# S5's tables in two sets of buffers with a later transpose, six tables loaded in the first FFN, and MoBA's bias rows written in 32 pieces

## The chip, the cores and the metric

One core of a Trainium2 chip runs the whole forward pass as one program. The metric is the device time of one execution in microseconds (us); lower is better. The core has five engines with an instruction stream each: PE (TensorE, matrix products; its weight loads are listed as PEld), DVE (VectorE), ACT (ScalarE), POOL (GpSimd) and SP (SyncE, which here only issues transfers). Each engine works through its own stream in order and waits on semaphores for the others. DRAM transfers (DMA) are issued from the queues of SP, ACT and POOL and run on 16 DMA engines. SBUF is the on-chip memory of 128 partitions, PSUM the accumulators that PE writes.

## What is computed

A model of four layers, width 1024, on one sequence of 256 tokens, in float32. Each layer is a feed-forward block (FFN, 1024 to 2816 to 1024), a mixer, and a second FFN. The mixers are S5 (a diagonal linear recurrence of 64 groups, 64 complex states and 16 channels each), HGRN2, GDN and MoBA (attention with a bias that depends on the distance, taken from a table of 32 buckets by 8 heads).

```python
def _swiglu(x, w_gate, w_up, w_down):
    return (jax.nn.silu(x @ w_gate) * (x @ w_up)) @ w_down

def _s5_mixer(u, lam_re, lam_im, log_dt, b_re, b_im, c_re, c_im, d_skip, w_glu):
    ...
    lam_bar = jnp.exp(lam * dt)
    b_bar = ((lam_bar - 1.0) / lam)[..., None] * lax.complex(b_re, b_im)
    bu = jnp.einsum('blgh,gph->lbgp', ug, b_bar)
    _, h = lax.associative_scan(combine, (a, bu), axis=0)      # h[l] = lam_bar * h[l-1] + bu[l]
    y = jnp.einsum('lbgp,ghp->blgh', h, c).real.reshape(bsz, L, D_MODEL)
    y = jax.nn.gelu(y + d_skip * u)
    val, gate = jnp.split(y @ w_glu, 2, axis=-1)
    return val * jax.nn.sigmoid(gate)

for i in range(DEPTH):                                          # 4 layers: S5, HGRN2, GDN, MoBA
    x = x + 0.5 * _swiglu(_rms(x, norm_g[i, 0]), ffn_w_gate[i, 0], ffn_w_up[i, 0], ffn_w_down[i, 0])
    x = x + mixer_i(_rms(x, norm_g[i, 1]))
    x = x + 0.5 * _swiglu(_rms(x, norm_g[i, 2]), ffn_w_gate[i, 1], ffn_w_up[i, 1], ffn_w_down[i, 1])
return _rms(x, final_norm_g)
```

## The kernel before

**Parts.** The program runs twelve parts in a row (PARTS): the FFN (0,0), S5, the FFN (0,1), the FFN (1,0), HGRN, and so on; MoBA is the last mixer. FFN (l,0) stands ahead of the mixer of layer l and FFN (l,1) behind it.

**Products.** Each float32 product is made of three matmuls of 512 columns (`wide`, lines 347 to 349), because a weight block is cut in two parts, `hi` and `lo = raw - hi`. `Weights.pump` loads raw blocks on SP's queue (L71, four raw buffers), ACT casts `hi` (L88) and VectorE subtracts `lo` (L91, 128x1024, both inputs in SBUF). An FFN is 66 steps of 12 such matmuls, 792 in all: 11 blocks of four steps for gate and up, then 22 steps for down. `hhl` is the hidden state, so the matmuls of gate and up read `xhl` and those of down read `hhl`. L459 stands once in each FFN near its start, L484 writes its result at the end. `step()` in `ffn` runs once per step; at its end it also calls `next(self.prep)`, at odd steps before the 32nd and at each step before the 60th.

**S5's tables.** `self.prep` is a generator (`s5_prep`) which lays the making of S5's matrices beside the first FFN, the only FFN that has it. It makes eight tables `j`, for 8 groups each. For one table POOL issues six operations of 128x512 (L732, L733 and L734, twice) into the second half of the buffer `s5e`, the halves `ebs`; VectorE issues three of 128x1024 (L737, L738, L740) into its first half `eo`; PE makes a block of 16 small matmuls (L746) from `eo` and eight transposes (L760) of `ebs`; ACT copies the transposes out of PSUM (L761); and SP writes `s5_out` (L741), for every fourth table `s5_k` (L754, 8 transfers), and `s5_in` (L762, 2 transfers) to DRAM. There is one buffer `s5e`, so POOL's L733 of the next table waits for the transposes of this one, and PE's transposes wait for POOL's L734. There are two `yield`s in a table. Behind the tables `s5_phases` makes the powers of the recurrence for the first half on POOL.

**S5.** `s5()` reads the tables back from DRAM with `load`, twelve tables of 1 MB (four each of `in`, `t` and `out`) in five buffers (tags A to E) that the preparation used before. `in` tables go into the scan's input (`inward`), `t` tables (L804, eight transfers each) and `out` tables into the output `y` (`to_y`, whose matmuls are listed at L882). POOL makes the phases of the second half and `xr` (L943), then two of the second scan's products (L898); VectorE's second scan follows and ends in the transposes L952, whose result PE transposes at L955. `busy` (L253) lays idle matmuls into a wait.

**The bias.** `moba_bias`, called in the first FFN after the preparation, that is FFN (0,1), behind its gate and up blocks in the program's text, reads the bias table, builds a row of 384 values per head on POOL, and writes it 128 times to DRAM, as 8x128x384 values (1536 KB), in one transfer on ACT's queue (L1719). A scheduler of the framework places the instructions on each engine by their dependences and a cost model, so an instruction's place need not be that of its line.

```python
pb = [back[:, n, h].unsqueeze(3).to_broadcast(wh) for n in range(2)]
g(tb[:, :4], b1[:, h].unsqueeze(2).to_broadcast(wh), pb[0], op=OP.mult)
g(split(eb), b2[:, h].unsqueeze(2).to_broadcast(wh), pb[1], op=OP.mult)
g(split(eb), split(eb), tb[:, :4], op=OP.add)
```

## Time and profile before

| what | value |
|---|---|
| median of 3 runs | 2255.6 us (2252.84 to 2257.62) |
| the profiled execution | 2255.48 us, its span in the profile 2253.7 us |
| mean granted TensorE clock | 0.982 of full speed |
| PE busy | 2147.5 us, 95% of the span, 11480 instructions |
| PEld busy | 1771.5 us, 79% |
| DVE busy | 1464.5 us, 65%, 2412 instructions |
| ACT busy | 1159.8 us, 51% |
| POOL busy | 288.1 us, 13%, 305 instructions |
| DMA | 389.63 MB, 173 GB/s in the mean |
| chain that ended last | PE 80%, DVE 9%, ACT 4%, DMA 3%, POOL 2% |

Busy shares are means over stages that differ. The chain of waits and the waits of PE tell where the end is set; the first 300 us and the FFN behind S5 are the two places that the change touches. All times below are from the start of the span.

### The profile page before, as it was taken

The numbers are of one execution on the slowest core, as the hardware profiler recorded it, in microseconds if no ns is written. First come the engines' busy times: TensorE is split into PE (matmuls) and PEld (weight loads), VectorE is DVE, ScalarE is ACT, GpSimd is POOL, SyncE is SP. The second block draws the span as 40 slices with busy tenths as digits, with TensorE's granted clock in tenths as the row PEclk, the third lists the DMA queues.
The fourth block names the chain that finished last, engine by engine and source line by source line (L and its number), as shares of the span: only waits on it lengthen the run. The fifth ranks groups of instructions, "written<-read, shape, count | busy, mean of one in ns | idle before, by whom it ended". The sixth has DMA issues, their size and how long they took to land.

```text
span 2253.7 us, 30309 instructions
## 1 busy us (share of the span) xinstructions
PE 2147.5 (95%) x11480; PEld 1771.5 (79%) x11480; DVE 1464.5 (65%) x2412; ACT 1159.8 (51%) x1876; POOL 288.1 (13%) x305
## 2 busy tenths in 40 slices
PE   8989888999999999999999888899999999999998
PEld 6767566888888888887888766777888888898886
DVE  7986675556555877557554888887655555666555
ACT  6444344445454755445444566764544544555443
POOL 0598600000000000001000422322000000000000
PEclk9999899999999999999999999999999999999999
DMA  8656956655555645555655433233555655555553
GB/s 254 195 188 203 239 185 166 191 195 179 186 179 185 198 132 169 187 190 167 190 185 175 144 100 104 85 113 121 179 187 172 202 186 178 196 168 178 187 177 103
DMA packets 317906, 389.63 MB, mean 173 GB/s; under 512 B 14192, under 2 KB 247856, under 8 KB 316736
## 3 DMA queue, kind: packets, MB, share of 16 engines
q1 hardware_dynamic: 314768, 383.92, 53.7%
q10 hardware_dynamic: 2800, 3.68, 0.9%
q8 instruction: 90, 1.47, 0.3%
q14 instruction: 56, 0.46, 0.1%
q0 software_dynamic: 192, 0.10, 0.0%
HBM read 375.65 MB, written 12.01 MB: 172 GB/s over the span
## 4 chain that ended last, share of the span: by engine, by line
PE 80%; DVE 9%; ACT 4%; DMA 3%; POOL 2%; issue 1%; SPq 0%; ACTq 0%; DVEq 0%; POOLq 0%
PE acc L349 23%; PE acc L347 23%; PE acc L348 23%; DVE lo L91 2%; PE acc L315 2%; PE acc L316 2%; PE acc L317 2%; PE aux L439 2%; DVE cy L1395 1%; DMA raw<-in_ffn_w_up_dram 1%; ACT hi L88 1%; PE aux L230 1%; POOL s5e L733 1%; POOL s5e L734 1%; POOL s5tmp L732 1%
## 5 line engine op out<-in xcount | busy, mean ns | idle before, releaser
L91 DVE TENSOR_TENSOR lo<-raw,hi 128x1024 fp32r<-128x1024 f32 x648 | 813.1, 1257 | 585.4 <-ACT hi L88 582.3
L88 ACT CAST hi<-raw 128x1024 fp32r<-128x1024 f32 x681 | 713.1, 1049 | 708.2 <-PE acc L349 657.5
L347 PE MATMUL acc<-hi,xhl 128*128 128x512 f32 x1568 | 627.2, 400 | 9.9 <-ACT hi L88 9.4
L348 PE MATMUL acc<-lo,xhl 128*128 128x512 f32 x1568 | 618.9, 395 | 2.8 <-DVE lo L91 2.7
L349 PE MATMUL acc<-hi,xhl 128*128 128x512 f32 x1568 | 616.9, 394 | 0.0
L347 PEld LDWEIGHTS acc<-hi,xhl 128*128 128x128 f32 x1568 | 297.1, 190 | 73.0 <-ACT hi L88 10.7
L349 PEld LDWEIGHTS acc<-hi,xhl 128*128 128x128 f32 x1568 | 296.9, 189 | 66.6 <-issue 3.1
L348 PEld LDWEIGHTS acc<-lo,xhl 128*128 128x128 f32 x1568 | 297.5, 190 | 64.4 <-DVE lo L91 5.2
L347 PE MATMUL acc<-hi,hhl 128*128 128x512 f32 x704 | 276.9, 393 | 0.0
L349 PE MATMUL acc<-hi,hhl 128*128 128x512 f32 x704 | 276.7, 393 | 0.0
L348 PE MATMUL acc<-lo,hhl 128*128 128x512 f32 x704 | 275.5, 391 | 0.0
L349 PEld LDWEIGHTS acc<-hi,hhl 128*128 128x128 f32 x704 | 132.8, 189 | 27.6
L348 PEld LDWEIGHTS acc<-lo,hhl 128*128 128x128 f32 x704 | 132.9, 189 | 27.4
L347 PEld LDWEIGHTS acc<-hi,hhl 128*128 128x128 f32 x704 | 132.7, 188 | 27.0
L317 PE MATMUL acc<-xhl,lo 128*128 128x256 f32 x520 | 150.2, 291 | 0.0
L316 PE MATMUL acc<-xhl,hi 128*128 128x256 f32 x520 | 149.5, 290 | 0.2 <-DVE xhl L241 0.2
L315 PE MATMUL acc<-xhl,hi 128*128 128x256 f32 x520 | 149.6, 291 | 0.1
L427 ACT ACTIVATE sl<-acc,norm_r 128x256 f32<-128x256 f32 x176 | 83.6, 475 | 107.2 <-PE acc L349 88.9
L91 POOL TENSOR_TENSOR lo<-raw,hi 128x1024 fp32r<-128x1024 f32 x33 | 81.8, 2478 | 342.7 <-ACT hi L88 322.6
L430 DVE TENSOR_TENSOR h<-acc,sl 128x256 f32<-128x256 f32 x176 | 74.0, 420 | 49.8 <-ACT sl L427 49.7
L315 PEld LDWEIGHTS acc<-xhl,hi 128*128 128x128 f32 x520 | 99.6, 193 | 2.6 <-issue 1.7
L316 PEld LDWEIGHTS acc<-xhl,hi 128*128 128x128 f32 x520 | 99.8, 193 | 1.6 <-issue 0.9
(564 smaller groups left out, 2285.7 us busy)
## 6 DMA issues: line engine op xcount, KB each, us to landing
raw<-in_ffn_w_gate_dram SPq DMA_DIRECT2D x174, 512.0 KB, 3.9
raw<-in_ffn_w_up_dram SPq DMA_DIRECT2D x174, 512.0 KB, 4.8
raw<-in_ffn_w_down_dram SPq DMA_DIRECT2D x80, 1024.0 KB, 4.9
raw<-in_gdn_w_in_dram SPq DMA_DIRECT2D x24, 1024.0 KB, 5.2
raw<-in_hg_w_in_dram SPq DMA_DIRECT2D x16, 1024.0 KB, 5.3
raw<-in_moba_w_in_dram SPq DMA_DIRECT2D x12, 1024.0 KB, 5.0
raw<-in_ffn_w_down_dram SPq DMA_DIRECT2D x16, 512.0 KB, 3.7
raw<-in_s_w_glu_dram SPq DMA_DIRECT2D x16, 512.0 KB, 5.2
```

The source lines that it names most:

```text
L88: pin(self.nc.scalar.copy(hi, src))
L91: eng.tensor_tensor(lo, src, hi.bitcast(F32), op=OP.subtract)
L230: nc.tensor.transpose(q[:, j * 128:j * 128 + 128], self.x[:, t, k * 128:k * 128 + 128], self.ident)
L315: t.matmul(p, hi, ah, start=first, stop=False)
L316: t.matmul(p, hi, al, start=False, stop=False)
L317: t.matmul(p, lo, ah, start=False, stop=last)
L347: mm(p, ah, hi[:, j], start=first and j == 0, stop=False)
L348: mm(p, ah, lo[:, j], start=False, stop=False)
L349: mm(p, al, hi[:, j], start=False, stop=last and j == n - 1)
L427: nc.scalar.activation(sl, p[:, :256], AF.Silu, scale=self.r_col[:, t:t + 1])
L430: return nc.vector.tensor_tensor(waiting[-1][1][:, t], p[:, 256:], sl, op=OP.mult)
L439: nc.tensor.transpose(q[:, c:c + 128], h[:, t, f * 128:f * 128 + 128], self.ident)
```

## The change

Three things are done. First, S5's tables alternate between two buffers, `s5e` and `s5f` (a new sixth tag, G), and the transposes of table j-1 (`turned`) are issued with table j, behind its 16 small matmuls; a table has three `yield`s, with two more around the last transposes, and the generator is stepped at odd steps before the 24th and at every step from there on. Second, a new method `s5_load` holds what `load` did, with six tags; the preparation calls it for six tables (`in` 0 to 3, `t` 0 and 1), with the phases of the first half between them, and `load` in `s5()` takes these before it loads others. Third, `moba_bias` is a generator: its first step builds the row, and each of 32 further steps writes 4 of the 128 copies (8x4x384 values, 48 KB) on ACT's queue, kept in program order; `ffn` steps it once per step from the fifth on, and `moba` finishes what is left. Docstrings and unrelated lines do not change.

```diff
--- before.py
+++ after.py
@@ -443,23 +443,26 @@
                 return nc.vector.tensor_tensor(hhl[:, 2 * j:2 * j + 2, 1], q, hh.bitcast(F32), op=OP.subtract)
 
             steps = [0]
+            bias = None
+            if self.prep is None and self.bias is not None:
+                bias = self.bias(pool)
+                self.bias = None
 
             def step():
                 steps[0] += 1
                 n = steps[0]
                 if n % 4 == 1 and waiting and n > 4:
                     turn()
+                if bias is not None and n > 4:
+                    next(bias, None)
                 if self.prep is not None and n > 4:
-                    for _ in range(n % 2 if n < 32 else 1 if n < 60 else 0):
+                    for _ in range(n % 2 if n < 24 else 1):
                         next(self.prep, None)
 
             for j in range(FT // 2):
                 self.product(self.xhl, KT // 2, lambda t, p: evac(j, t, p), tail=0 if j else 4, step=step)
             half = self.small.tile([128, 2], F32, name="half")
             nc.vector.tensor_scalar(half, self.r_col, 0.5, None, op0=OP.mult)
-            if self.prep is None and self.bias is not None:
-                self.bias(pool)
-                self.bias = None
             ahead = self.ahead
 
             def late():
@@ -708,7 +711,9 @@
         for n in range(8):
             nc.gpsimd.tensor_copy(back[:, :, :, n], pw[:, :, :, 8 - n])
         e = pool.tile([128, 16, 128], F32, name="s5e", tag="s5C")
-        eo, ebs = e[:, :8], (e[:, 8:12], e[:, 12:16])
+        more = pool.tile([128, 16, 128], F32, name="s5f", tag="s5G")
+        eos = e[:, :8], more[:, :8]
+        ebs = [(t[:, 8:12], t[:, 12:16]) for t in (e, more)]
         w = [128, 8, 8, 16]
         split = lambda a: a.rearrange("p g (t h) -> p g t h", h=16)
         ta, tb = [tmp[:, c].rearrange("p (g t h) -> p g t h", t=8, h=16) for c in range(2)]
@@ -721,13 +726,23 @@
                                     pattern=[[128 * sign, 2], [0, 4], [-8 * sign, 32]], channel_multiplier=sign)
         self.s5_place = pool.tile([128, 16], F32, name="s5place")[:, :8]
         v.tensor_reduce(self.s5_place, self.ident.rearrange("p (a t) -> p t a", t=8), op=OP.add, axis=mybir.AxisListType.X)
+        def turned(j):
+
+            for n, eb in enumerate(ebs[j % 2]):
+                p = self.aux.tile([128, 512], F32, name="aux")
+                for g in range(4):
+                    nc.tensor.transpose(p[:, g * 128:g * 128 + 128], eb[:, g], self.ident)
+                nc.scalar.copy(et.rearrange("p g c -> p (g c)"), p)
+                dma(as_ap(self.s5_in, (8 * j + 4 * n) * 128, [[8192, 128], [128, 4], [1, 128]]), et)
+
         for j in range(8):
             r = slice(8 * j, 8 * j + 8)
-
-            rs = (slice(8 * j, 8 * j + 4), slice(8 * j + 4, 8 * j + 8))
-            for h, eb in zip(rs, ebs):
+            eo = eos[j % 2]
+
+            for n, eb in enumerate(ebs[j % 2]):
+                h = slice(8 * j + 4 * n, 8 * j + 4 * n + 4)
                 wh = [128, 4, 8, 16]
-                pb = [back[:, n, h].unsqueeze(3).to_broadcast(wh) for n in range(2)]
+                pb = [back[:, m, h].unsqueeze(3).to_broadcast(wh) for m in range(2)]
                 g = nc.gpsimd.tensor_tensor
                 g(tb[:, :4], b1[:, h].unsqueeze(2).to_broadcast(wh), pb[0], op=OP.mult)
                 g(split(eb), b2[:, h].unsqueeze(2).to_broadcast(wh), pb[1], op=OP.mult)
@@ -739,6 +754,7 @@
             yield
             v.tensor_tensor(split(eo), split(eo), ta, op=OP.add)
             dma(as_ap(self.s5_out, j * 1024, [[8192, 128], [128, 8], [1, 128]]), eo)
+            yield
 
             p = self.aux.tile([128, 512], F32, name="aux")
             for g in range(2):
@@ -753,21 +769,26 @@
                         a = q * 32 + g * 16
                         dma(as_ap(self.s5_k, (8 * (j - 3) + 2 * q + g) * 3840 + 112, [[240, 16], [8 * 3840, 4], [1, 128]]),
                             kk[a:a + 16, :, g])
+            if j:
+                turned(j - 1)
             yield
-            for h, eb in zip(rs, ebs):
-                p = self.aux.tile([128, 512], F32, name="aux")
-                for g in range(4):
-                    nc.tensor.transpose(p[:, g * 128:g * 128 + 128], eb[:, g], self.ident)
-                nc.scalar.copy(et.rearrange("p g c -> p (g c)"), p)
-                dma(as_ap(self.s5_in, h.start * 128, [[8192, 128], [128, 4], [1, 128]]), et)
-
+        yield
+        turned(7)
+        yield
+
+        self.s5_tags = ["s5" + c for c in "ABCDEG"]
+        self.s5_tabs = []
         self.s5_turn = pool.tile([128, 2, 16, 32], F32, name="s5turn", tag="s5pw")
-        yield from self.s5_phases(self.s5_turn, 0, pool)
+        phases = self.s5_phases(self.s5_turn, 0, pool)
+        for kind, part in (("in", 0), ("in", 1), ("in", 2), ("in", 3), ("t", 0), ("t", 1)):
+            self.s5_tabs.append(self.s5_load(kind, part))
+            next(phases, None)
+            yield
 
     def s5_phases(self, turn, half, pool):
 
         eng = self.nc.gpsimd
-        t2 = pool.tile([128, 2, 16, 8], F32, name="s5t2", tag="s5F")
+        t2 = self.s5_pool.tile([128, 2, 16, 8], F32, name="s5t2", tag="s5F")
         pin = self.tc.keep_in_program_order
         pin(eng.memset(turn[:, 0, :, 0:1], 1.0))
         pin(eng.memset(turn[:, 1, :, 0:1], 0.0))
@@ -782,6 +803,21 @@
                           [t2[:, c, :, :n] for c in range(2)], eng)
             yield
 
+    def s5_load(self, kind, part):
+
+        tags = self.s5_tags
+        tags.append(tags.pop(0))
+        t = self.s5_pool.tile([128, 16, 128], F32, name="tab", tag=tags[-1])
+        if kind == "t":
+
+            for s in range(8):
+                self.nc.sync.dma_start(t[s * 16:s * 16 + 16],
+                                       as_ap(self.s5_k, part * 16 * 3840 + (7 - s) * 16, [[240, 16], [3840, 16], [1, 128]]))
+        else:
+            src = self.s5_in if kind == "in" else self.s5_out
+            self.nc.sync.dma_start(t, as_ap(src, part * 2048, [[8192, 128], [128, 16], [1, 128]]))
+        return t.rearrange("p (j q g) c -> p j q g c", q=4, g=2)
+
     def s5_token(self, k):
 
         self.nc.vector.transpose(self.s5_u[:, k].rearrange("p g t h -> p t g h"),
@@ -792,21 +828,12 @@
         v = nc.vector
         mm = nc.tensor.matmul
         pin = self.tc.keep_in_program_order
-        tags = ["s5" + c for c in "ABCDE"]
+        tags = self.s5_tags
 
         def load(kind, part):
-
-            tags.append(tags.pop(0))
-            t = self.s5_pool.tile([128, 16, 128], F32, name="tab", tag=tags[-1])
-            if kind == "t":
-
-                for s in range(8):
-                    nc.sync.dma_start(t[s * 16:s * 16 + 16],
-                                      as_ap(self.s5_k, part * 16 * 3840 + (7 - s) * 16, [[240, 16], [3840, 16], [1, 128]]))
-            else:
-                src = self.s5_in if kind == "in" else self.s5_out
-                nc.sync.dma_start(t, as_ap(src, part * 2048, [[8192, 128], [128, 16], [1, 128]]))
-            return t.rearrange("p (j q g) c -> p j q g c", q=4, g=2)
+            if self.s5_tabs:
+                return self.s5_tabs.pop(0)
+            return self.s5_load(kind, part)
 
         with ExitStack() as ctx:
             pool = ctx.enter_context(self.tc.tile_pool(name="s5", bufs=1))
@@ -1716,7 +1743,11 @@
             nc.gpsimd.tensor_copy(row[:, lo:hi], tab[:, b:b + 1].to_broadcast([8, hi - lo]))
 
         self.bias_rows = self.dram.tile([8, 128, 384], F32, name="bias_rows")
-        nc.scalar.dma_start(self.bias_rows, row.rearrange("h (o s) -> h o s", o=1).to_broadcast([8, 128, 384]))
+        for k in range(0, 128, 4):
+            yield
+            self.tc.keep_in_program_order(nc.scalar.dma_start(
+                as_ap(self.bias_rows, k * 384, [[128 * 384, 8], [384, 4], [1, 384]]),
+                row.rearrange("h (o s) -> h o s", o=1).to_broadcast([8, 4, 384])))
 
     def moba(self, i):
         nc = self.nc
@@ -1725,7 +1756,7 @@
         with self.tc.tile_pool(name="moba", bufs=1) as pool, self.tc.tile_pool(name="moba2", bufs=2) as two:
             bt = pool.tile([128, H, L], F32, name="bt")
             if self.bias is not None:
-                self.bias(pool)
+                self.settle(self.bias(pool))
 
             nc.scalar.dma_start(bt, as_ap(self.bias_rows, 127, [[383, 128], [128 * 384, H], [1, L]]))
             qk = pool.tile([128, 2, H, L], F32, name="qk")
```

On POOL, at the start of the tables in the first FFN, the stream before was this (`s5D` and `s5kk` are inputs, `s5tmp` the first product, `s5e` the table buffer):

```order
L709 COPY s5kk<-s5pw 128x128 x8
L732 TENSOR_TENSOR s5tmp<-s5D,s5kk 128x512
L733 TENSOR_TENSOR s5e<-s5D,s5kk 128x512 x2
L734 TENSOR_TENSOR s5e<-s5e,s5tmp 128x512
L732 TENSOR_TENSOR s5tmp<-s5D,s5kk 128x512
L734 TENSOR_TENSOR s5e<-s5e,s5tmp 128x512
```

With the change it is this:

```order
L712 COPY s5kk<-s5pw 128x128 x8
L747 TENSOR_TENSOR s5tmp<-s5D,s5kk 128x512
L748 TENSOR_TENSOR s5e<-s5D,s5kk 128x512 x2
L749 TENSOR_TENSOR s5e<-s5e,s5tmp 128x512
L748 TENSOR_TENSOR s5f<-s5D,s5kk 128x512
L747 TENSOR_TENSOR s5tmp<-s5D,s5kk 128x512
L748 TENSOR_TENSOR s5f<-s5D,s5kk 128x512
L749 TENSOR_TENSOR s5e<-s5e,s5tmp 128x512
```

The same six operations per table remain, 48 in all; writes to the second buffer stand among those to the first. On PE the last transposes of the tables (L760 before, L734 now) stand behind 629 of the FFN's 792 wide matmuls before, and behind 664 with the change.

On SP, at the end of the first FFN and ahead of S5, the stream before was this (`tab` with its number is a table that S5 reads; `raw` blocks of `in_s5_w_glu` are S5's weights):

```order
L741 DMA s5_out_1203<-s5e_1215 128x1024
L754 DMA s5_k_1204<-s5kk_1206 16x4x128 x8
L762 DMA s5_in_1202<-s5tmp_1009 128x512
...
L808 DMA tab_2325<-s5_in_1202 128x2048
L71 DMA raw_2076<-in_s5_w_glu_dram 128x4x256 x2
L808 DMA tab_2344<-s5_in_1202 128x2048
...
L804 DMA tab_2454<-s5_k_1204 16x16x128 x8
L804 DMA tab_2481<-s5_k_1204 16x16x128 x8
L808 DMA tab_2531<-s5_out_1203 128x2048
```

With the change it is this:

```order
L770 DMA s5_k_1118<-s5kk_1120 16x4x128 x8
L736 DMA s5_in_1116<-s5tmp_939 128x512
...
L818 DMA tab_1970<-s5_in_1116 128x2048
L736 DMA s5_in_1116<-s5tmp_939 128x512
...
L818 DMA tab_2055<-s5_in_1116 128x2048
L71 DMA raw_2067<-in_s5_w_glu_dram 128x4x256 x2
L814 DMA tab_2082<-s5_k_1118 16x16x128 x7
L814 DMA tab_2125<-s5_k_1118 16x16x128 x8
L71 DMA raw_2138<-in_s5_w_glu_dram 128x4x256 x2
```

The `in` tables and the first `t` table stood ahead of or among S5's weight loads already, since the scheduler had drawn them forward. The first `in` table now stands ahead of the last writes of `s5_in`, and the second `t` table comes ahead of S5's last weight loads.

On ACT, at the end of S5 and the start of FFN (0,1), the one transfer stood here before (L240 normalises, L88 casts weights):

```order
L246 ACTIVATE junk_3160,ssq_2822<-x_81 128x512
L240 ACTIVATE xhl_2821<-aux_3147,gains_95 128x128
L1719 DMA bias_rows_4161<-row_4133 1024x1x384
L240 ACTIVATE xhl_2821<-aux_3147,gains_95 128x128
L427 ACT_TABLE_LOAD
```

With the change the first pieces stand in the FFN's steps, one per step, between the casts:

```order
L442 CAST hhl_3191<-aux_3296 128x2x256
L1748 DMA bias_rows_3333<-row_3305 8x4x384
L88 CAST hi_3351<-raw_3098 128x1024
L1748 DMA bias_rows_3333<-row_3305 8x4x384
L88 CAST hi_3371<-raw_3202 128x1024
```

Each piece also waits for the semaphore that the fourth piece before it signals, so at most four are under way, and a piece that waits holds up the casts behind it on ACT.

## Rows read from the trace of the kernel before

**Rows 1.** Waits of PE in 0 to 500 us (engine, tile, line <- releaser: total us, times, longest).

```profile
PE acc L882 <- DMA tab<-s_k: 11.6, 3, 5.0
PE aux L760 <- POOL s5e L734: 10.9, 5, 2.7
PE acc L347 <- ACT hi L88: 8.1, 2, 7.4
PE aux L746 <- DVE s5e L740: 4.5, 2, 3.1
```

**Rows 2.** Windows (us, busy of PE, PEld, DVE, ACT, POOL; clock, DMA share, GB/s).

```profile
40.00:80.00 40.00, 38.45 (x191) 30.86 (x190) 38.08 (x128) 25.90 (x38) 5.64 (x9) 1.00 0.56 170
260.00:290.00 30.00, 18.13 (x298) 12.78 (x299) 23.92 (x33) 3.24 (x6) 20.58 (x25) 0.76 1.15 236
```

**Rows 3.** Lines by form, 109.3 to 204.9 us (count | busy us, mean ns | idle before, releaser).

```profile
L91 DVE TENSOR_TENSOR lo<-raw,hi 128x1024 fp32r<-128x1024 f32 x22 | 38.9, 1769 | 16.5 <-ACT hi L88 16.5
L734 POOL TENSOR_TENSOR s5e<-s5e,s5tmp 128x512 f32<-128x512 f32 x16 | 29.6, 1852 | 0.6
L733 POOL TENSOR_TENSOR s5e<-s5D,s5kk 128x512 f32<-128x512 f32 x16 | 27.5, 1736 | 9.8 <-PE aux L760 9.8
L732 POOL TENSOR_TENSOR s5tmp<-s5D,s5kk 128x512 f32<-128x512 f32 x16 | 27.3, 1705 | 1.3
...
L740 DVE TENSOR_TENSOR s5e<-s5e,s5tmp 128x1024 f32<-128x1024 f32 x7 | 13.2, 1883 | 0.1
L738 DVE TENSOR_TENSOR s5e<-s5E,s5pw 128x1024 f32<-128x1024 f32 x7 | 12.8, 1833 | 0.6 <-PE aux L746 0.3 <-DMA s_out<-s5e 0.2
L737 DVE TENSOR_TENSOR s5tmp<-s5E,s5pw 128x1024 f32<-128x1024 f32 x6 | 11.1, 1855 | 0.0
```

**Rows 4.** Timeline of POOL in the tables (start us, us, engine, line, operation).

```profile
109.35 1.05 POOL L732 TENSOR_TENSOR s5tmp<-s5D,s5kk 128x512 f32<-128x512 f32 x1
...
136.11 4.04 POOL L733 TENSOR_TENSOR s5e<-s5D,s5kk 128x512 f32<-128x512 f32 x2
...
169.68 2.07 POOL L733 TENSOR_TENSOR s5e<-s5D,s5kk 128x512 f32<-128x512 f32 x2
171.71 1.28 POOL L734 TENSOR_TENSOR s5e<-s5e,s5tmp 128x512 f32<-128x512 f32 x1
...
202.71 2.13 POOL L734 TENSOR_TENSOR s5e<-s5e,s5tmp 128x512 f32<-128x512 f32 x1
```

**Rows 5.** Timeline of DVE, one table operation with POOL idle.

```profile
182.65 1.22 DVE L737 TENSOR_TENSOR s5tmp<-s5E,s5pw 128x1024 f32<-128x1024 f32 x1
```

**Rows 6.** Timeline of PE, behind the last table and at the FFN's end.

```profile
205.62 0.40 PE L347 MATMUL acc<-hi,hhl 128*128 128x512 f32 x1
...
244.19 0.60 PE L936 MATMUL acc<-zero 128*128 128x512 bf16 x2
```

**Rows 7.** Timeline of POOL, DVE and PE in S5, around the second scan.

```profile
278.63 2.49 POOL L898 TENSOR_TENSOR tb<-inc,turn 128x512 f32<-128x512 f32 x2
...
288.61 1.30 DVE L952 STREAM_TRANSPOSE sc<-S 128x512 f32<-128x512 f32 x2
...
292.01 0.81 PE L955 MATMUL aux<-ident,sc 128*128 128x128 f32 x3
```

**Rows 8.** Lines L459 and L484, 300 to 600 us, and L484, 600 to 900 us (durations, starts).

```profile
L459 DVE TENSOR_SCALAR half<-norm_r x2: 169/169/169, 351.0 to 548.8; 128x2 f32<-128x2 f32 x2
...
L484 DVE SCALAR_TENSOR_TENSOR x<-acc,half,x x4: 744/746/750, 510.4 to 543.3; 128x512 f32<-128x512 f32 x4
...
L484 DVE SCALAR_TENSOR_TENSOR x<-acc,half,x x4: 743/746/751, 697.7 to 730.7; 128x512 f32<-128x512 f32 x4
```

**Rows 9.** Transfers (KB each, us to landing): 345 to 390 us; 0 to 500 us.

```profile
raw<-in_ffn_w_up_dram SPq DMA_DIRECT2D x6, 512.0 KB, 15.1
...
s_in<-s5tmp SPq DMA_DIRECT2D x16, 256.0 KB, 3.0
```

**Rows 10.** Timeline of ACT's queue, the bias transfer's issue.

```profile
350.43 0.79 ACTq L1719 DMA_DIRECT2D bias_rows<-row  x1
```

## The prediction

> **What bounds the kernel now.** I read PE's waits first, then the windows, then the groups of lines in the stretch where the tables are made, then single rows of the timeline. The waits list says where PE stood still in the first 500 us [rows 1]: 11.6 us for S5's `t` tables, 10.9 us in the transposes of the tables for POOL's L734, 8.1 us for a cast on ACT (7.4 of it in one piece), 4.5 us in the small matmuls for VectorE's L740. These are what the three parts of the change aim at. But a wait that is taken away is worth only what no other work takes over, so for each I look at what ends next.
>
> *First FFN, tables.* The tables run from 109.35 to 204.84 us [rows 4], 95.5 us. The reader should see in [rows 3] that L732, L733 and L734 on POOL take about 1.7 to 1.85 us each and VectorE's L91, L737, L738 and L740 about 1.8 to 1.9. The same operations alone are far shorter: on POOL the two L733 at 169.68 take 2.07 us together and L734 1.28, against 4.04 for two L733 at 136.11 [rows 4]; L737 takes 1.22 on VectorE while POOL is idle [rows 5]. So the two engines slow each other when both run. Counted together, there are 48 operations on POOL and 22 + 7 + 7 + 6 = 42 on VectorE [rows 3], 90 in 95.5 us, 1.06 us each, nearly what each takes alone. The two engines behave almost like one, and that one has hardly any room: the waits of PE and POOL's 9.8 us behind PE's transposes [rows 3] lie beside VectorE's half of that work. *S5.* In 260 to 290 us POOL is busy for 20.6 of 30 us and VectorE for 23.9, PE for 18.1 with a granted clock of 0.76 [rows 2]. *The bias.* FFN (0,1) runs from L459 at 351.0 to the last L484 at 543.3, 192.3 us; FFN (1,0), the same work without a bias, from 548.8 to 730.7, 181.9 us [rows 8]. The excess is 10.4 us.
>
> **The sum** is made against the profiled execution, 2255.48 us (its span 2253.7); the median of the runs is 2255.6, so the two can be taken as one.
>
> *1. Tables with a second buffer, PE one step behind.* Nothing is added to the tables' arithmetic: 48 operations on POOL, 24 on VectorE, as many transposes, copies and writes. POOL starts a little later: with the change one more table operation of VectorE stands ahead of POOL's copies, and VectorE has 38.08 us of work in the 40 before [rows 2], so I take about one such operation, 1.14 us (1.22 [rows 5] less what consecutive operations overlap): 110.49. From there VectorE has 17 table operations rather than 20 beside POOL, since three more of them come earlier, but 25 splits rather than 22, because PE uses more weights by then. Again 90 operations at 1.06 us, so 95.5 us: POOL ends at 205.98. What is gained is that PE does not stand by. In the order the last transposes are reached after 664 wide matmuls, not after 629, so 128 and not 163 are left. PE resumed 0.78 us after POOL's end, at 205.62, and the FFN ended at 244.19 [rows 6]: 38.57 us for 163 matmuls, so 30.3 us for 128. The FFN then ends at 205.98 + 0.78 + 30.3 = 237.1 rather than 244.2: **-7.1 us**. Bounds: if every operation costs what it does alone and they strictly follow each other, POOL's 48 at (1.05 + 1.03 + 1.28)/3 = 1.12 make 53.8 us and VectorE's 42 at 1.22 make 51.2, 105.0 together, and the FFN ends at 246.6, +2.4. At the other end PE's 10.9 and 4.5 us of waits go altogether, -15.4. I take the value between, since it uses the rate that this very stretch had, waits and all.
>
> The Trainium skill, page "SBUF — State Buffer", section "Who interferes with whom", says that a VectorE instruction with two SBUF inputs contends with a POOL instruction that reads SBUF, over a port pair that is an exclusive lock. Taken strictly, it speaks against this change: by it the second buffer can't overlap the two engines, and the stretch would be the 105.0 us above rather than 95.5. The trace agrees that they contend, though 95.5 us with idle time in it is less than the strict sum.
>
> *2. Six tables loaded in the first FFN.* In the order before, the four `in` tables and the first `t` table already stand at the FFN's end, drawn there by the scheduler; only the second `t` table really moves ahead. The 11.6 us of waits for `t` tables are three, and the third lies in the second half. Behind them PE does not end S5: POOL's L898 runs to 281.12, then VectorE's second scan ends in L952, at 288.61 and the first half done at about 289.3, and PE takes its result at 292.01 [rows 7]. So at most 292.0 - 289.3 = 2.7 us can come off; the rest of the 11.6 is hidden behind POOL and VectorE. A loss is possible too: PE now idles in other places and its clock, 0.76 in the mean there, may be low where the chain needs it; the three transposes at 292.01 took 0.81 us [rows 7], and I allow that much again, +0.8. I take **-1.4**, half the gain, since one of the three waits is fully covered and two are not. SP's queue has six more waits ahead of S5's weight loads (on the buffers' last readers), but those weights are used behind the scans.
>
> *3. Bias in 32 pieces.* Weight loads issued beside the one transfer of 1536 KB took 15.1 us to land [rows 9], a cast waited for one, and PE for the cast 7.4 us [rows 1]; the excess of 10.4 us [rows 8] is that wait and what PE lost at a lower clock behind it. Pieces of 48 KB can't hold the 16 DMA engines for long: 256 KB land in 3.0 us [rows 9]. The 32 issues cost ACT up to 0.79 us each [rows 10], 25 us in all, but ACT is busy 25.9 of 40 us in an FFN [rows 2] and the issues lie in its idle time; I leave one, 0.8 us, on the path: **-9.6**. If ACT had no room, they'd cost more, see the last rival. Bounds: the 7.4 us wait alone, or all 10.4.
>
> The Trainium skill, page "DMA: Bandwidth & Descriptors", section "Bandwidth", says to batch transfers to 1 MiB or more, and that those under 64 KB are dominated by descriptors; by it the pieces speak against this part. No run here shows pieces of this form yet.
>
> Sum: -7.1 - 1.4 - 9.6 = -18.1, so 2255.5 - 18.1 = **2237.4 us**.
>
> **Rivals.** *(a) VectorE and POOL strictly one after the other*: the first term is +2.4, so 2255.5 + 2.4 - 1.4 - 9.6 = 2246.9. For it: alone against together in [rows 4, 5]. Against it: the 95.5 us. *(b) The loop is bound by PE's waits*: all 15.4 us go, 2255.5 - 15.4 - 1.4 - 9.6 = 2229.1. For it: POOL idles 9.8 us for PE, and VectorE's splits wait 16.5 us for ACT's casts [rows 3]. Against it: operations become slower the more they overlap. *(c) S5 gets all 11.6 us back*: 2255.5 - 7.1 - 11.6 - 9.6 = 2227.2; against it stands the chain over POOL and VectorE [rows 7]. *(d) Slower: pieces block ACT.* A piece waits for the one four before, on ACT's in-order queue, ahead of the casts that PE needs. An FFN has 66 steps in 181.9 us, 2.76 us each, one piece per step. If a piece takes more than 4 x 2.76 = 11.0 us to land, the FFN follows the pieces: at the 15.1 us that the weights had beside the big transfer, 3.78 us a piece, 1.02 more than a step, 32 times 32.6 us. Then the third term is -10.4 + 32.6 = +22.2 and the time 2255.5 - 7.1 - 1.4 + 22.2 = 2269.2. Against it: [rows 9], small stores landing in 3.0 us. *(e) The change doesn't do what it says*: for four or five of the six tables it doesn't, as the order shows; that is in the sum.
>
> **Numbers.** The forecast has a chance of 0.57, (a) 0.18, (b) 0.12, (c) 0.07, (d) 0.06. The time is the likeliest case's, 2237.4. The range reaches from (c) at 2227 to (a) with the bias at its small end, 2246.9 + 2.2 = 2249; (d), and what the bounds don't hold, lie outside. 0.2% is about 4.5 us, what a measurement of this kernel can tell from no change. All cases but (d) are faster by more; I give 0.90 faster, 0.04 the same (a loop at its worst end with S5's loss and half the bias's gain), 0.06 slower.
>
> **What would show it.** Right: the first FFN ends near 237 us with POOL's tables ending near 206, and the waits for L734 and L740 are gone while the means of L91 and L733 stay near 1.8; S5 is one to two us shorter and still waits for POOL's L898; the FFN behind S5 takes about 183 us with no cast waiting 7 us, and weight loads land in about 5 us. Wrong: POOL's last table ends far from 206 either way; the pieces land later than 11 us and casts on ACT wait for them; or S5 shortens by more than 2.7 us, which would mean that its chain ran over PE.

## The result and the profile after

The changed kernel takes 2243.0 us (median of 4 runs, 2242.12 to 2243.31) against 2255.0 us, a ratio of 0.9946 with a 95% interval of 0.9928 to 0.9963: 12 us faster, where 18.1 were forecast. The profiled execution has a span of 2240.8 us.

The program was cut at three points that both traces have: PE's first zero matmul behind the first FFN (L936 before, L963 now), PE's second product of S5's output (the L347 on `yhl` that waits for `ysum` on ACT), and the last result L484 or L487 of FFN (0,1).

| us | forecast | before | after | change |
|---|---|---|---|---|
| first FFN, to its end | -7.1 | 244.2 | 243.2 | -1.0 |
| S5, to the second product | -1.4 | 59.4 | 57.3 | -2.1 |
| rest of S5 and FFN (0,1) | -9.6 | 239.7 | 228.4 | -11.3 |

That is 14.3 us; the spans differ by 12.9. The instructions behind stand in the same order in both, and a stretch among them, between the last L484 at 1241.5 and 1227.2 and the next at 1735.0 and 1722.5, took 493.5 before and 495.3 after, and 491.7 to 495.5 in the profiles of the experiments, so this is the scatter of that stretch.

The waits of PE after, in 0 to 500 us, which answer to [rows 1]:

```profile
PE aux L982 <- DVE sc L979: 10.5, 2, 6.1
PE aux L734 <- POOL s5e L749: 8.9, 2, 7.5
...
PE aux L734 <- DVE hhl L443: 2.8, 1, 2.8
...
PE acc L909 <- DMA tab<-s_k: 0.5, 1, 0.5
```

Of the four waits that were aimed at, three are nearly gone from the list; the fourth remains, as PE still waits 8.9 us for POOL, 7.5 of it at the first table. In S5 the 11.6 us for tables have become 10.5 us for VectorE. So the list got shorter by much more than the time did.

The waits of ACT in 100 to 250 us, before and after (two lines of each), show a wait that is new:

```profile
ACT hi L88 <- PE acc L349: 60.9, 30, 7.0
...
ACT s5tmp L761 <- DMA s_in<-s5tmp: 0.2, 1, 0.2
```

```profile
ACT hi L88 <- PE acc L349: 34.3, 21, 3.9
ACT s5tmp L735 <- DMA s_in<-s5tmp: 19.6, 7, 5.2
```

Before a transposed table is copied out of PSUM (L735), the one copy buffer `et` must have been written to DRAM. That was so before as well, but there the casts on ACT waited 60.9 us for PE, and the writes landed in that time. Now those waits are 34.3 us and ACT waits for the writes. The chain that ended last, from 181 to 210 us, runs over just that (its 15 longest pieces):

```profile
181.69 0.38 SPq L71
182.16 5.86 DMA s_in<-s5tmp
188.10 0.60 ACT s5tmp L735
188.71 1.96 DMA s_in<-s5tmp
190.75 0.60 ACT s5tmp L735
191.36 5.14 DMA s_in<-s5tmp
196.61 0.60 ACT s5tmp L735
197.22 3.80 DMA s_in<-s5tmp
201.10 0.60 ACT s5tmp L735
201.71 4.15 DMA s_in<-s5tmp
206.10 0.34 issue
206.44 1.06 ACT hi L88
207.53 1.22 DVE lo L91
208.75 0.67 DVE x L487
209.56 0.94 PE aux L230 x4
```

Five writes and four copies follow each other, at 2 to 6 us a write. Weight loads and the first table loads are under way beside the writes; which of them makes a write long is not shown. The weight cast at 206.44 stands behind the copies on ACT's in-order queue, the split and the result behind it on VectorE, and PE at the end. On PE, and on POOL, the timeline shows the same place and the tables' first and last operations:

```profile
206.32 0.40 PE L348 MATMUL acc<-lo,hhl 128*128 128x512 f32 x1
209.56 0.94 PE L230 MATMUL aux<-ident,x 128*128 128x128 f32 x4 [2.84 <-DVE x L487]
...
212.86 0.75 PE L734 MATMUL aux<-ident,s5f 128*128 128x128 f32 x4
213.36 0.48 PE L348 MATMUL acc<-lo,hhl 128*128 128x512 f32 x1
...
243.23 0.82 PE L963 MATMUL acc<-zero 128*128 128x512 bf16 x3
```

```profile
114.46 1.92 POOL L747 TENSOR_TENSOR s5tmp<-s5D,s5kk 128x512 f32<-128x512 f32 x1
...
202.75 2.29 POOL L749 TENSOR_TENSOR s5f<-s5f,s5tmp 128x512 f32<-128x512 f32 x1
```

The tables start 5.1 us later than in [rows 4] and end at 205.0, as before. PE is past the last transposes at 213.4, 7.7 us later than in [rows 6], and has 30 rather than 38.6 us of work left.

In S5 the timeline of POOL, VectorE and PE answers to [rows 7]:

```profile
277.63 2.50 POOL L925 TENSOR_TENSOR tb<-inc,turn 128x512 f32<-128x512 f32 x2
...
287.62 1.31 DVE L979 STREAM_TRANSPOSE sc<-S 128x512 f32<-128x512 f32 x2
288.39 1.97 PE L982 MATMUL aux<-ident,sc 128*128 128x128 f32 x8 [6.08 <-DVE sc L979]
```

From the first FFN's end POOL's L925 starts 34.4 us later in both kernels, and VectorE's L979 44.4 us later in both; only PE, which came to the transposes at 47.8, is now there early, waits 6.1 us and goes on at 45.2. What held PE there before stands behind its last table:

```profile
286.76 1.94 PE L882 MATMUL acc<-tab,ut 128*32 128x128 f32 x32 [4.99 <-DMA tab<-s_k]
288.62 3.60 PE L253 MATMUL aux<-zero 128*128 128x512 bf16 x8
```

PE had used the last `t` table at 288.7, before VectorE's first half was done at 289.3. The eight idle matmuls of `busy`, which stand in the program's order behind that table, then kept it until 292.0. After the change the same eight run from 280.4 and take 1.90 us.

FFN (0,1) and FFN (1,0) answer to [rows 8]:

```profile
L465 DVE TENSOR_SCALAR half<-norm_r x2: 169/169/169, 348.4 to 534.4; 128x2 f32<-128x2 f32 x2
...
L487 DVE SCALAR_TENSOR_TENSOR x<-acc,half,x x4: 740/742/751, 496.0 to 529.0; 128x512 f32<-128x512 f32 x4
...
L487 DVE SCALAR_TENSOR_TENSOR x<-acc,half,x x4: 741/744/751, 683.4 to 716.3; 128x512 f32<-128x512 f32 x4
```

Between the marks FFN (0,1) now takes 180.6 us (192.3 before), FFN (1,0) 181.9 as before. Weight loads beside the pieces land as fast as elsewhere (transfers issued in 345 to 430 us), which answers to [rows 9]:

```profile
raw<-in_ffn_w_gate_dram SPq DMA_DIRECT2D x14, 512.0 KB, 3.9
```

### The profile page after: what moved, and what is told of

Its sections match the earlier page's. It is cut to its first block, busy times and chain, and to the rows that moved or that the text cites. A ratio compares the mean times of both kernels' runs of the same rounds, so it can differ in the third digit from the quotient of the medians.

```text
span 2240.8 us, 30340 instructions
## 1 busy us (share of the span) xinstructions
PE 2146.3 (96%) x11480; PEld 1775.4 (79%) x11480; DVE 1466.6 (65%) x2412; ACT 1159.2 (52%) x1876; POOL 296.4 (13%) x305
## 4 chain that ended last, share of the span: by engine, by line
PE 80%; DVE 10%; ACT 4%; POOL 2%; DMA 2%; issue 2%; SPq 0%; ACTq 0%; DVEq 0%; POOLq 0%
PE acc L347 23%; PE acc L349 23%; PE acc L348 23%; DVE lo L91 2%; PE acc L315 2%; PE acc L316 2%; PE acc L317 2%; PE aux L439 2%; DVE cy L1422 1%; DMA s_in<-s5tmp 1%; PE aux L230 1%; ACT hi L88 1%; DMA tab<-s_k 1%; POOL s5l L674 1%; ACT zb L1545 1%
## 5 line engine op out<-in xcount | busy, mean ns | idle before, releaser
L91 DVE TENSOR_TENSOR lo<-raw,hi 128x1024 fp32r<-128x1024 f32 x648 | 817.8, 1265 | 537.6 <-ACT hi L88 535.7
L88 ACT CAST hi<-raw 128x1024 fp32r<-128x1024 f32 x681 | 712.5, 1049 | 653.2 <-PE acc L349 617.2
L347 PE MATMUL acc<-hi,xhl 128*128 128x512 f32 x1568 | 623.0, 399 | 1.9 <-ACT hi L88 1.4
L347 PEld LDWEIGHTS acc<-hi,xhl 128*128 128x128 f32 x1568 | 296.6, 189 | 64.0 <-ACT xhl L240 2.0
L347 PE MATMUL acc<-hi,hhl 128*128 128x512 f32 x704 | 276.4, 393 | 0.0
L347 PEld LDWEIGHTS acc<-hi,hhl 128*128 128x128 f32 x704 | 132.3, 188 | 27.1
L91 POOL TENSOR_TENSOR lo<-raw,hi 128x1024 fp32r<-128x1024 f32 x33 | 82.0, 2483 | 341.0 <-ACT hi L88 321.0
L430 DVE TENSOR_TENSOR h<-acc,sl 128x256 f32<-128x256 f32 x176 | 74.0, 420 | 63.3 <-ACT sl L427 63.3
```

Source lines behind the costliest of these rows:

```text
L88: pin(self.nc.scalar.copy(hi, src))
L91: eng.tensor_tensor(lo, src, hi.bitcast(F32), op=OP.subtract)
L347: mm(p, ah, hi[:, j], start=first and j == 0, stop=False)
L430: return nc.vector.tensor_tensor(waiting[-1][1][:, t], p[:, 256:], sl, op=OP.mult)
```

## The experiments

Twelve kernels were run, each beside the kernel before. The first theory: the bias gives its gain alone; in S5 and the first FFN a new wait takes most of what the tables could give, and that wait is the single copy buffer. The rival: VectorE and POOL, slowed by each other, set the first FFN, whatever waits. All that follows is cut at the same three points, in the profiled execution of each kernel; the last two columns are lengths:

| kernel | median us | ratio [95%] | first FFN's end | S5 | FFN (0,1) |
|---|---|---|---|---|---|
| bias alone | 2244.9 | 0.9947 [0.9933, 0.9961] | 244.7 | 59.1 | 228.5 |
| tables and loads alone | 2253.2 | 0.9989 [0.9980, 0.9999] | 242.7 | 57.3 | 238.8 |
| change + second copy buffer | 2236.1 | 0.9915 [0.9901, 0.9929] | 236.9 | 57.3 | 228.5 |
| change + POOL in order | 2242.4 | 0.9945 [0.9932, 0.9957] | 242.1 | 57.0 | 228.4 |
| both of these | 2236.2 | 0.9912 [0.9898, 0.9925] | 239.0 | 57.3 | 228.5 |
| copy buffer, old pace | 2239.3 | 0.9927 [0.9914, 0.9939] | 240.0 | 57.1 | 228.4 |
| copy buffer, no early loads | 2236.5 | 0.9915 [0.9902, 0.9929] | 237.9 | 56.9 | 228.4 |
| the same, five buffers | 2236.3 | 0.9912 [0.9900, 0.9925] | 238.2 | 56.7 | 228.4 |
| copy buffer, s5l on ACT | 2241.8 | 0.9943 [0.9929, 0.9957] | 242.1 | 57.2 | 228.4 |
| before, bias in 8 pieces | 2244.7 | 0.9952 [0.9939, 0.9966] | 246.5 | 58.1 | 228.7 |
| before, bias 24 steps later | 2255.3 | 0.9993 [0.9984, 1.0002] | 243.7 | 58.7 | 236.6 |
| before + second copy buffer | 2256.6 | 1.0003 [0.9994, 1.0012] | 249.1 | 57.6 | 239.7 |

**The bias alone.** Only the third part of the diff was applied to the kernel before.

```diff
-        nc.scalar.dma_start(self.bias_rows, row.rearrange("h (o s) -> h o s", o=1).to_broadcast([8, 128, 384]))
+        for k in range(0, 128, 4):
+            yield
+            self.tc.keep_in_program_order(nc.scalar.dma_start(
...
+                if bias is not None and n > 4:
+                    next(bias, None)
```

> The kernel before with the bias written in 32 pieces and nothing else. Theory, by the stages of the two traces (from PE's second product of S5's output to the end of FFN (0,1), 239.7 us before and 228.4 after): the bias is worth 11.3 us by itself, so 2244 to 2246 us, with the first FFN ending at 244.2 as before. Rival: the part of it beyond the removed wait of 7.4 us comes from the earlier end of S5 and its weight loads, then 2247 to 2249 us.

It came out as the theory said, 0.9947, and the FFN is as long as in the full change. PE's wait for a cast on ACT (L88), 8.1 us in 0 to 500 us [rows 1], is 0.7 us.

**The tables and the loads alone**: the third part taken back, against the change.

```diff
-                if bias is not None and n > 4:
-                    next(bias, None)
...
+        nc.scalar.dma_start(self.bias_rows, row.rearrange("h (o s) -> h o s", o=1).to_broadcast([8, 128, 384]))
```

> The changed kernel with the bias written in one transfer as before. Theory: the tables and the early loads give 1.0 us in the first FFN and 2.1 us in S5, so 3 us in all, about 2252 us. Rival: the parts help each other and the tables alone give nothing, 2254 to 2256 us; or they give the forecast's 8.5 us, 2246 to 2247 us.

0.9989, 2253.2 us. The parts add up within the scatter: 11 and 3 us alone, 12 us together.

**A second copy buffer**, in a slice of the S5 input buffer that only the FFN's end writes:

```diff
-        et = tmp[:, 1, 512:].rearrange("p (g c) -> p g c", g=4)
+        ets = [tmp[:, 1, 512:].rearrange("p (g c) -> p g c", g=4),
+               self.s5_u[:, 6:8].rearrange("p k a t h -> p (k a t h)").rearrange("p (g c) -> p g c", g=4)]
...
+                et = ets[n]
```

> The changed kernel with a second buffer for the copies of the transposes (the second half of each table goes through a slice of the buffer for S5's input, which is idle until the FFN's end). Theory (the one copy buffer is the new wait): ACT's 19.6 us of waiting for the writes of s_in go, and with them PE's stall of 3.2 us from 206.3 us and its low clock behind it; the first FFN ends near 239 us and the time is about 2238 to 2240 us. Rival (VectorE and POOL share the SBUF port and set the pace): PE stalls for as long at another place, the first FFN ends within 1 us of 243.2, the time is 2242 to 2244 us.

The first FFN ends at 236.9 us, 6.3 earlier, more than the theory asked for, and the run is 7 us faster than the change. ACT's wait and PE's place behind the last table:

```profile
ACT s5tmp L736 <- DMA s_in<-s5tmp: 3.2, 2, 1.6
```

```profile
205.78 1.07 PE L734 MATMUL aux<-ident,s5f 128*128 128x128 f32 x8
206.60 0.48 PE L347 MATMUL acc<-hi,hhl 128*128 128x512 f32 x1
...
236.91 0.59 PE L964 MATMUL acc<-zero 128*128 128x512 bf16 x2
```

19.6 us became 3.2, and PE goes on at 206.6 rather than 213.4. PE's early 8.9 us are still there, so they were not what the change lost.

**POOL kept in the program's order.**

```diff
-                g = nc.gpsimd.tensor_tensor
+                g = lambda *a, **k: self.tc.keep_in_program_order(nc.gpsimd.tensor_tensor(*a, **k))
```

> The changed kernel with POOL's six operations of each table kept in the order of the program, so that table 0 is finished before table 1 begins. Theory (the copy buffer sets the end of the tables): PE's wait for L749 falls from 8.9 to about 4 us, POOL ends the tables near 205 us as before, and the first FFN ends less than 2 us earlier: 2241 to 2243 us. Rival (the early wait of 7.5 us is what the FFN lost): the FFN ends 4 to 5 us earlier, 2238 to 2239 us.

The wait fell to 5.1 us and the first FFN ended 1.1 us earlier: the theory, as far as so small a step shows it. (The first FFN of the kernel before, unchanged, ended at 243.7 to 246.5 us in four profiles.)

**Both together**: the last two diffs.

> The second copy buffer and POOL's program order together. Theory (once the copy buffer no longer sets the end, the early wait for table 0 counts): PE's wait for the tables falls from 8.9 to about 5 us as with the order alone, and the first FFN ends 2 to 4 us earlier than with the copy buffer alone, at 233 to 235 us; time 2232 to 2235 us. Rival (the shared SBUF port is the bound now): the FFN ends at 236 to 237 us again, time 2235 to 2237 us.

A miss: the first FFN ended at 239.0, later than with the copy buffer alone, and the time is the same. PE's waits for POOL are 7.4 us (L747 for `s5e`) and 2.4 (for `s5f`) and so no less than 8.9. The longest fell to 5.1 us, as with the order alone, but PE then waited for later tables.

**The old pace**, with the second copy buffer.

```diff
-                    for _ in range(n % 2 if n < 24 else 1):
+                    for _ in range(n % 2 if n < 32 else 1):
```

> The second copy buffer, and the generator stepped at the pace of the kernel before (odd steps up to the 32nd). Theory (VectorE's table operations, drawn ahead by the faster pace, slow POOL's copies of s5l and s5kk, so that the tables start at 114.5 and not at 109.4 us): the tables start near 110 us again and PE doesn't wait for table 0; the first FFN ends 2 to 5 us earlier than 236.9 us, time 2231 to 2235 us. Rival (the sum of the operations sets it): the tables start earlier but end where they did, near 206 us, and PE reaches the last transposes with the same work left, so the FFN ends within 1 us of 236.9.

A miss for both: the tables start at 113.4 rather than 114.6, so the pace is only 1.2 us of what makes them late; they end near 210 and the FFN ends 3.1 us later. PE doesn't wait for table 0, but 10.0 us for L430 (`h`) and 5.7 for L487.

**No early loads**, with the second copy buffer.

```diff
-        for kind, part in (("in", 0), ("in", 1), ("in", 2), ("in", 3), ("t", 0), ("t", 1)):
-            self.s5_tabs.append(self.s5_load(kind, part))
+        for _ in range(6):
             next(phases, None)
```

> The second copy buffer without the six early loads: all twelve tables are loaded by S5 itself, still from six buffers. Theory (the scheduler had drawn five of the six loads forward anyway, only the second t table moves): the first FFN ends as with the copy buffer alone, 236 to 238 us, and S5 up to PE's second product of its output takes at most 2 us more than 57.3 us; time 2236 to 2239 us. Rival (the early loads are what S5 gained, and the sixth buffer gives nothing): S5 takes 2 us more, 59 to 60 us, and the t waits of 11.6 us are back.

Not slower than with them, 2236.5 against 2236.1, and S5 took 56.9 us. So S5's 2.1 us are not the early loads', and the rival falls. The remaining candidate was the sixth buffer.

**Five buffers**: the last kernel with one tag less.

```diff
-        self.s5_tags = ["s5" + c for c in "ABCDEG"]
+        self.s5_tags = ["s5" + c for c in "ABCDE"]
```

> As the kernel without early loads, but S5's tables go through five buffers (A to E) and not six; the second copy buffer stays. Theory (S5 gains by the sixth buffer, not by the early loads, since S5 took 56.9 us without them): S5, from the first FFN's end to PE's second product of its output, takes 59 to 60 us as in the kernel before, the three waits for t tables come back with 11 to 12 us, the time is 2 us above that kernel's, about 2238 to 2239 us. Rival (the earlier end of the tables' making helps S5's loads): S5 stays at 57 us, time 2236 to 2237 us.

The t waits came back and S5 did not get longer. The first FFN ends at 238.2 us, and VectorE's L979 starts 44.1 us behind that, as in the other kernels. PE's waits, and PE at the end of S5:

```profile
PE acc L909 <- DMA tab<-s_k: 11.4, 3, 4.5
```

```profile
279.62 1.94 PE L909 MATMUL acc<-tab,ut 128*32 128x128 f32 x32 [4.50 <-DMA tab<-s_k]
281.89 1.89 PE L253 MATMUL aux<-zero 128*128 128x512 bf16 x7 [0.33 <-issue]
283.62 1.04 PE L982 MATMUL aux<-ident,sc 128*128 128x128 f32 x8
```

That theory falls too, and the rival's numbers hold; its reason is not shown. 11.4 us of PE's waits for tables, in a kernel as fast as without them, cost nothing. What counts is when PE is through the third of these tables and the idle matmuls behind it. Before, that table's use starts 42.6 us behind the FFN's end, the idle matmuls take 3.60 us, and PE comes to L955 3.4 us behind the start of VectorE's L952. Here it starts at 41.4, they take 1.89 us, and PE comes 1.3 us behind: still a little later than VectorE, which has the first half ready at 283.0. The granted clock was 0.53, close to the lower of its two levels, in 286.7 to 293.0 us before, and 0.75 in 279.6 to 285.0 here. Ahead of the third table PE frees the buffers for these loads 2 us earlier here, as its fourteen idle matmuls at S5's start took 3.18 us, not 5.80, at a granted clock of 1.00 against 0.54. Whether that is the whole reason for the earlier table was not tried.

So S5's length here goes with the clock as well as with the tables. With the S5 of the kernel before, the profiles of the bias alone, the 8 pieces, the later transfer and the second copy buffer have 57.6 to 59.1 us, so the 59.4 of the kernel before is the longest of five, and the change's gain against the other four is about 0.2 to 1.7 us. No run leaves out the idle matmuls.

**The bias in 8 pieces** of 192 KB, one in four steps, against the kernel with the bias alone.

```diff
-        for k in range(0, 128, 4):
-            yield
+        for k in range(0, 128, 16):
+            for _ in range(4):
+                yield
```

> The kernel before with the bias written in 8 pieces of 192 KB, one in four steps. Theory (only the size of what stands in the DMA engines ahead of a weight load counts, and 192 KB is little against the four raw buffers): the same as 32 pieces, 2243 to 2246 us. Rival (pieces must be as small as 48 KB): a piece delays weight loads by 3 to 4 us, casts wait, and half of the gain is lost, 2248 to 2251 us.

The same as 32: 228.7 against 228.5 us.

**The bias in one transfer, later**, 24 steps into the FFN, against the same.

```diff
-        for k in range(0, 128, 4):
-            yield
+        for k in range(0, 128, 128):
+            for _ in range(24):
+                yield
```

> The kernel before with the bias in one transfer of 1536 KB as before, but issued 24 steps later in the same FFN. Theory (the size of the transfer holds up weight loads wherever it stands): weight loads beside it take 14 to 15 us, a cast waits, the FFN is 8 to 11 us longer than with pieces, time 2252 to 2256 us. Rival (the place hurt: at the FFN's start nothing is buffered, later four raw blocks and split parts cover it): most of the gain without any pieces, 2244 to 2247 us.

Its time is that of the kernel before within the interval, which leaves room for at most 3.6 us. In its trace the FFN takes 236.6 us, and ACT's timeline and PE's waits in 0 to 560 us have the old pattern:

```profile
459.55 1.04 ACT L88 CAST hi<-raw 128x1024 fp32r<-128x1024 f32 x1 [13.16 <-DMA raw<-in_ffn_w_up_dram]
```

```profile
PE acc L347 <- ACT hi L88: 4.4, 1, 4.4
```

The cast waits 13.2 us, and PE 4.4, not 7.4. So the size is what costs, 8.1 us of FFN (0,1) against the pieces. The 3.1 us by which FFN (0,1) is shorter than before stand in this one profile; the medians differ by 0.9 us, so that the place is worth anything is not shown.

**The second copy buffer in the kernel before**: `et = ets[n]` in its loop, with the same `ets` as above.

> The kernel before with only the second copy buffer. Theory (the copy buffer binds only when the transposes are a step behind, ACT waited 0.2 us for it in the kernel before): no change, 2254 to 2257 us, first FFN's end at 243.5 to 245 us. Rival (the copy buffer is worth as much by itself): 2248 to 2250 us.

No gain, 1.0003; in its profiled execution, one of its longest at 2260.6 us, the FFN even ended at 249.1, later than was expected. So the copy buffer binds only when the transposes come a step late, which is what this change made.

**The copies of s5l on ACT**, to begin the tables earlier, with the second copy buffer.

```diff
-                    nc.gpsimd.tensor_copy(self.s5_l[q * 32:q * 32 + 32, n]...
+                    nc.scalar.copy(self.s5_l[q * 32:q * 32 + 32, n]...
```

> The second copy buffer, and the 24 small copies of s5l on ACT rather than on POOL. Theory (POOL's copies ahead of the tables, 14.2 us of them from 87 us, set the tables' late start at 114.5 us and with it PE's 8.9 us of waiting for table 0): the tables start at 100 to 104 us, PE does not wait for table 0, POOL ends the tables near 195 us and the first FFN ends 5 to 9 us earlier than 236.9 us; time 2227 to 2232 us. Rival (the whole of the two-input work on VectorE and POOL sets the FFN, and PE catches up only with it): the tables start earlier, but PE waits as long for splits or later tables, the FFN ends within 2 us of 236.9, time 2234 to 2237 us.

Theory and rival both fell: the tables started at 106.3, 8.3 us earlier than with the copy buffer alone, yet ended at 208.0 rather than 206.1, and the FFN ended at 242.1, 5.2 us later.

```profile
106.29 2.02 POOL L748 TENSOR_TENSOR s5tmp<-s5D,s5kk 128x512 f32<-128x512 f32 x1
...
205.82 2.16 POOL L750 TENSOR_TENSOR s5f<-s5f,s5tmp 128x512 f32<-128x512 f32 x1
```

```profile
PE aux L439 <- DVE h L430: 16.6, 9, 3.8
```

```profile
POOL s5f L749 <- PE aux L734: 7.1, 1, 7.1
```

PE waits 16.6 us for VectorE, and POOL 7.1 for PE: a new order of the three engines, with as much waiting in another place. The tables' stretch held 94 operations of the two engines in 101.7 us, against 87 in 91.6 with the copy buffer alone: about the same time for each (1.08 and 1.05 us), but more of VectorE's operations lay in it. What would let the tables run through faster stays open.

## Why the prediction was right, and where it was wrong

**The direction and the range held**; the size was too large by 6 us, all of it in the first term. The other two came out slightly larger than forecast. The bias alone gives 11 of the 12 us, so the direction is right by the third part, and hardly by the tables.

**The first FFN, -7.1 forecast, -1.0 measured.** The rate was right: from 114.46 to 205.04 POOL did its 48 operations and VectorE 38 of the two-input kind (22 of L91, 16 of the tables, by the groups of lines in that stretch), 86 in 90.6 us, 1.05 each where the forecast used 1.06; 664 wide matmuls stood ahead of the last transposes. That POOL ended at 205.0, where 206.0 was said, is chance: it started 4.0 us later than forecast, and four fewer operations of VectorE lay in the stretch.

Of the sum, the step that failed is "Nothing is added to the tables' arithmetic: 48 operations on POOL, 24 on VectorE, as many transposes, copies and writes" and "What is gained is that PE does not stand by". The copies and writes are as many, but they were costed at nothing, and no cover was named for them. Before, the waits of ACT show them covered by its 60.9 us of waiting for PE. Now the transposes of a table come behind its successor, that cover is 34.3 us, and two copies and two writes of each table go one after the other through one buffer, at 2 to 6 us a write, with 19.6 us of ACT's time lost. The casts behind them made PE stand by 2.8 us at 206.7 us and go on at a low granted clock (0.79 in 206 to 214 us), so that it passed the last transposes at 213.4, not at 206.8. With a second copy buffer PE went on at 206.6 and the FFN ended at 236.9, where the forecast had 206.8 and 237.1. That the forecast's working describes that kernel so closely is in part chance, too: the tables started 5 us later than before and not 1.1. In the change POOL's copies ahead of them took 14.2 and 7.05 us where they had taken 12.2 and 6.0, beside VectorE's operations that the second buffer lets through earlier. PE's 8.9 us of waiting for POOL, 7.5 of it at the first table, were not in the sum either.

**S5, -1.4 forecast, -2.1 measured**, inside the bound of 2.7. The bound was right: PE came to the second transposes 2.7 us earlier, and then took 0.6 us longer to the second product, at a granted clock of 0.87 against 0.97. That most of the 11.6 us of waits cost nothing, as forecast, the five-buffer kernel shows outright. Two reasons were not right. The 2.7 us were laid to the wait for tables, but PE was through with them before VectorE was ready, and the idle matmuls behind them filled that time. And the second `t` table, taken as the one real move, isn't needed for the gain. That the gain is over 1.4 is in part luck, since the S5 of the kernel before scatters by almost 2 us over five profiles.

**The bias, -9.6 forecast, -11.3 measured**, outside its bound of 10.4. The mechanism was right: without the transfer's 7.4 us wait the granted clock of FFN (0,1) is 1.00 throughout, where it was 0.76 in 371 to 391 us. The bound came from FFN (1,0) as a likeness of FFN (0,1) without the bias; between the same marks FFN (0,1) takes 180.6 us without the wait, 1.3 less than FFN (1,0).

**The rivals.** (a), strict alternation, asked for 105 us in the tables; by its own prices the 86 operations that lay there would take 53.8 + 38 x 1.22 = 100.2 us, and the 90.6 measured speak against it. Its outcome for the FFN, no gain, came about by another way. (b), the loop bound by PE's waits for the tables, is refuted by the old pace: there PE doesn't wait for POOL at all, and the FFN ends later, with the waits moved to VectorE. (c), all 11.6 us of S5, is refuted as those waits went and S5 gained 2.1. (d), pieces blocking ACT, did not happen: PE waits for no cast in FFN (0,1), the loads beside the pieces landed in 3.9 us, and 8 pieces and 32 gave the same. The Trainium skill, page "DMA: Bandwidth & Descriptors", section "Bandwidth", speaks for transfers of 1 MiB and against those under 64 KB; by that rule the pieces should have cost time. The runs don't agree (0.9947 with the pieces alone): nothing waits for the bias transfer's own rate, but weight loads landed in 15.1 us beside it and in 3.9 beside the pieces.

**What is left open**: what sets the first FFN at about 237 us once the copies are free (three tries at it, the order, the pace and the early start, made it end later). The arithmetic of VectorE and POOL together, at 1.05 to 1.10 us an operation in every profile here, is the likelier limit, but no run takes operations away. Whether the copy buffer would bind without the early loads, whose transfers run beside the last writes, and what S5 takes without the idle matmuls behind its last `t` table, was not tried either.

The best kernel run is the change with the second copy buffer: 2236.1 us, 0.9915 [0.9901, 0.9929] of the kernel before, and 7 us below the change. Without the early loads and the sixth buffer it is as fast, 2236.3.

## What to carry to other kernels

When a producer and a consumer are set a step apart with a second buffer, look at every buffer on the way behind them as well, down to the one that a DMA empties: the narrowest one sets the new step, and an engine that waits for it in order takes everything behind it along (here the weight casts). A wait that is long in the list may cost nothing: compare the moment at which the other chain needs the result, and expect only that difference. A large transfer beside a stream of small, timely ones is best cut into pieces with one due at a time; between 48 and 192 KB the size of a piece did not matter here. Idle work that is placed to fill a wait has to be looked at again when the wait moves: in order behind a late input, it holds up what comes next.

## What was not expected

The write of a 256 KB block to DRAM took from 1.96 to 5.86 us in one kernel within 25 us, among 1 MB weight loads and table loads, where the median was 3.0 in the kernel before and 2.3 in this one. Operations with two SBUF inputs on VectorE slowed even POOL's small copies (8 of 128x128 took 6.0, 7.05 and 10.0 us in three kernels): over all the profiles, one of them took 0.42 to 0.46 us with no such operation beside it, and 1.41 to 1.49 when it lay mostly beside one. And the kernel's later, unchanged stages scatter by almost 4 us (491.7 to 495.5 in one stretch), as much as the smaller parts of such a change are worth.
